# Two more tiles of a feed-forward layer as seven block products, with the work around them moved

## The chip, the cores and the metric

The kernel runs on one core of a Trainium2 chip. The metric is device time in microseconds (us): the median of several executions. One further execution is recorded by the hardware profiler. Its page and its trace are what is read here. The engines are called as in the profile: PE is TensorE (matmuls), PEld its weight loads, DVE is VectorE, ACT is ScalarE, POOL is GpSimd, and SP issues most of the DMAs.

## The reference

One layer of a streaming encoder (model width 1024) is computed for two groups of columns: 1024 positions of a new stream and 32 of a running one. A modulated input goes through one input projection into three kinds of heads, their outputs through an output projection and a layer norm; then comes a gated feed-forward layer of width 2816 and a second layer norm. The change lies in the feed-forward layer:

```python
x = _layer_norm(ALPHA * x + (1 + g1) * mix, ln1_g, ln1_b)
h = x * (1 + sc2) + sh2
y = (jax.nn.silu(h @ w_gate) * (h @ w_up)) @ w_down
x = _layer_norm(ALPHA * x + (1 + g2) * y, ln2_g, ln2_b)
```

`silu(v)` is `v * sigmoid(v)`. All of it is float32.

## The kernel before

**Layout.** Activations lie transposed: 128 partitions by 8 blocks `k` of the model width, with positions along the free axis. The 1056 positions are cut into group 0 (512 columns) and group 1 (544 columns). Every product of a weight `W` and an activation `x` is made of three matmuls on rounded parts, `W_hi x_hi + W_hi x_lo + W_lo x_hi` (function `gemm`, lines L130, L131, L132). Weights are loaded in float32, cast to their high part by ACT (L117) and split off to their low part by DVE (L118).

**The feed-forward stage.** `w_gate` and `w_up` are cut into 22 tiles `j` of 128 output rows (`FF = 22`). The function `up` makes one such tile directly: for each of its two column ranges a gate product and an up product over 8 blocks `k`, then `silu` on ACT and DVE (L1310 to L1315), which leaves the high and low part of the tile's activation. In group 1 the ranges are 0 to 272 and 272 to 544, so a direct tile has 2 matrices x 8 blocks x 3 parts x 2 ranges = 96 matmuls of 272 columns.

The function `sup` makes the same tile from seven block products (a scheme of Strassen's kind for a 2 by 2 block matrix with four `k` blocks each): 7 x 4 x 3 = 84 matmuls. For that it needs sums of weight blocks and sums of activation blocks. The weight sums are formed partly in advance, in DRAM, by `sums()`: SP copies one block (L90, tile name `start_dp`), and a DMA issued by POOL adds another onto it (L1333). The rest of a tile's weight sums are two DVE additions (L1387, L1388), and three casts and splits (L1381, L1382). The activation sums, called the operand `T`, are formed once by `sup_operand`: the feed-forward input was stored to DRAM block by block (`start_dh<-lna_tmp`), and is loaded back in pairs (blocks `k` and `k+4`); for each of four pairs DVE makes four additions of 272 columns (L1356 to L1359) and two splits of 544 (L1362). The seven products are combined by DVE (L1408 to L1422), out of two PSUM tags that alternate.

In group 1, tiles 0, 1 and 2 are direct (`SJ = 3`), 3 to 20 go by block products, and the last one (`TS = 1`) is direct.

**Order of the work.** Group 0 runs the whole feed-forward layer first, then group 1. Tiles are taken in `GROUPS` of 3, 3, 4, 4, 4 and 4; one tile beyond a group is made before the group's `down` product, which adds `w_down` times the tiles' activations into the residual `z` (DVE updates at L1212). So for group 1: tiles 0 to 3, down of tiles 0 to 2, tiles 4 to 6, down of tiles 3 to 5, and so on.

Two pieces of work are tied to the place where group 0 ends and group 1 begins. First, the last `down` of group 0 calls `ln_sum` for each of its outputs: ACT squares `z` (L1073), DVE adds the squares into `qs` (L1074), POOL adds `z` into `zs` (L1083). Two matmuls with a matrix of ones make means of these (`ln_means`, L1095, tile `lnb_t`), from which the second layer norm of group 0 (`ln2`, a generator `norm0`) goes on, step by step, behind tiles from 3 on, as the list `turns` says. Second, `ln1_res(1)` scales and shifts group 1's residual, 16 instructions `tensor_scalar` on POOL (L1268), each 128 by 272; `down` of group 1 adds onto them later.

Each engine runs its own queue in order; waits are semaphores on other engines and DMAs. The order within each queue is made by a scheduler from the program's dependences and from a model of time; `issue_after` adds an order without a wait.

Of the kernel before, what the change touches and what calls it, by code (L numbers as in the profile page):

```python
# [15 lines left out]
P = 128  # L16
D = 1024
KT = 8
# [28 lines left out]
FF = 22  # L47
SJ = 3
TS = 1
# [19 lines left out]
class Kernel:  # L69
    def __init__(self, ctx, tc, d):  # L70
        self.ctx, self.tc, self.nc, self.d = ctx, tc, tc.nc, d
        self.n = 0
        self.phase = "start"

    def pool(self, name, bufs=1, ctx=None, **kw):
# [22 lines left out]
    def tie(self, ins, target, engines):  # L98
        for i in ins:
            if i.engine in engines and "DMA" not in type(i).__name__ and "Dma" not in type(i).__name__:  # L100
                self.tc.add_manual_dep(i, target.ins.name, mybir.DependencyInfo(
                    mybir.DependencyClass.NoSync, mybir.DependencyReason.SCHED_ONLY), reason="order")

    def weights(self, src, nk, ncol, eng=None, pool=None):
# [958 lines left out]
    def ln_sum(self, st, z, m, sl):  # L1063
# [5 lines left out]
        if st["last"] and m != o[7]:  # L1069
            sq = self.t((self.pg, self.pu)[m % 2], [P, 512], F32, self.utag[m % 2])[:, :sl.stop - sl.start]  # L1070
        else:
            sq = self.t(self.p2, [P, 272], F32, "tmp", 4)[:, :sl.stop - sl.start]
        nc.scalar.activation(sq, z[:, m, sl], AF.Square)  # L1073
# [187 lines left out]
    def ln1_res(self, c):  # L1261

        self.phase = f"lna{c}"
        for a, b in MM[c]:
            for k in range(KT):
                zk = self.z[c][:, k, a:b]
# [3 lines left out]
                else:  # L1270
                    self.nc.scalar.activation(zk, zk, AF.Identity, bias=self.colp[:, 56 + k:57 + k],
                                              scale=self.colp[:, 48 + k:49 + k])

    def ln_consts(self):
# [59 lines left out]

    def sup_operand(self, ks):

# [6 lines left out]
        def load(k):  # L1343
            self.phase = "sup"
            x, y = ((self.t(self.px, [P, 544], F32, z, 1) for z in ("c", "uv")) if k % 2 else
                    (f(self.t(self.px, [P, 544], F32R, z, 1)) for z in ("w2h", "w2l")))
# [3 lines left out]

        loaded = {k: load(k) for k in ks[:2]}
        yield
        for k in ks:
# [6 lines left out]
            for z, (h, l) in zip((x, y), self.T):  # L1360
                nc.scalar.copy(h[:, k], z)
                tt(l[:, k], z, f(h[:, k]), ALU.subtract)  # L1362
            if k + 2 in ks:
                loaded[k + 2] = load(k + 2)
            yield
# [219 lines left out]
    def run(self):  # L1585
# [147 lines left out]
        with ExitStack() as s7:  # L1733
            pq = self.pool("pq", ctx=s7)
            for u, h in enumerate(range(PRE, 8)):
                self.fm_unit(w3[1 + h], self.evac_qk(h, True), (1,))
                if u:
                    self.ada((18 + 2 * u, 19 + 2 * u), pq, "late", 6, self.pt, "t")
        self.ln1_res(0)
        s1.close()  # L1740
# [9 lines left out]
        for g, (j0, nj) in enumerate(GROUPS):  # L1750
# [31 lines left out]
            else:  # L1782
                self.down(0, g, act, WIDE)
        st.update(pivot=False, sum=True)
        self.down(0, last, act, MM[0], st)
        self.ln1_res(1)
        self.st0 = st
# [3 lines left out]
        self.px = self.pool("px")  # L1791
        operand = self.sup_operand(range(4))
        next(operand)
# [5 lines left out]
        norm0 = norm0()  # L1799
        turns = [1, 1, 2, 2, 2, 1] * 2  # L1800
        for g, (j0, nj) in enumerate(GROUPS):
            for j in range(j0 + (g > 0), min(j0 + nj + (g < last), FF - TS)):
                if self.nsum <= FF:
                    self.sums()
                if j >= SJ:
                    self.sup(j, act, pa)
                    with tc.issue_after(self.lastact.ins):
                        for _ in range(turns.pop(0) if turns else 0):
                            next(norm0, None)
                    continue  # L1810
                for i, _ in enumerate(self.up(1, j, act, pa, MM[1])):
                    if 0 < 2 * j + i // 2 < 5 and i % 2:
                        with tc.issue_after(self.lastact.ins):
                            next(operand, None)
            if g < last:
# [135 lines left out]
```

## Time and profile before

| | us |
|---|---|
| median of 3 runs | 1334.09 (1333.72 to 1335.16) |
| the profiled execution | 1336.75 |
| its span, first to last instruction | 1334.6 |

The mean granted clock of PE was 0.997. On one core every engine's time line can be read directly: the span, then who is busy, then who waits for whom. Times in the quoted rows count from the span's start. In PE's rows, the end of group 0's last `down` comes at about 946.5 us, tiles 0 to 3 of group 1 follow until about 993, and the `down` of tiles 0 to 2 after them.

### The profile page before, as it was taken

The page shows a single profiled execution, that of the slowest core. Times are in us where ns is not written, and L with a number is a line of the kernel's source. Part 1 is how long each engine was busy: PE and PEld are TensorE (multiplying, and loading weights), DVE is VectorE, ACT ScalarE, POOL GpSimd, SP SyncE. Part 2 cuts the span into 40 slices and gives each one's busy share as a digit, 9 for nine tenths or more (in the row PEclk, how much of TensorE's full clock was granted, in tenths as well). Part 3 has the DMA queues.
Part 4 walks back from the last instruction along what each step waited for, and adds up shares of the span by engine and source line. Part 5 has one row for each costly group of instructions (what it writes and reads, how often), then busy time and mean ns, then how long its engine had stood idle before and what let it go on. Part 6 is the DMA issues. An engine that isn't in the chain of part 4 may idle for free.

```text
span 1334.6 us, 24982 instructions
## 1 busy us (share of the span) xinstructions
PE 1319.4 (99%) x9424; PEld 1196.9 (90%) x9424; DVE 989.6 (74%) x2106; ACT 647.2 (48%) x1284; POOL 183.7 (14%) x221
## 2 busy tenths in 40 slices
PE   9999999999999999999999999999999999999996
PEld 6798888978999888888887888999999999999996
DVE  4636666667778677777777676778998997978677
ACT  3424456443537645455354454436754463635344
POOL 0101100011305000000000001134600000000423
PEclk9999999999999999999999999999999999999998
DMA  9775555533748655354343334663786866644311
GB/s 362 276 257 167 182 180 180 152 130 111 222 169 258 186 136 147 112 163 115 111 139 108 102 104 129 202 146 113 207 219 161 233 177 188 177 139 136 102 49 67
DMA packets 118135, 217.43 MB, mean 163 GB/s; under 512 B 18340, under 2 KB 62496, under 8 KB 118016
## 3 DMA queue, kind: packets, MB, share of 16 engines
q1 hardware_dynamic: 111200, 204.37, 48.9%
q0 software_dynamic: 5616, 10.86, 4.9%
q8 instruction: 74, 1.21, 0.4%
q10 hardware_dynamic: 1200, 0.62, 0.2%
q14 instruction: 45, 0.37, 0.1%
HBM read 184.95 MB, written 50.77 MB: 177 GB/s over the span
## 4 chain that ended last, share of the span: by engine, by line
PE 90%; DMA 4%; DVE 3%; ACT 1%; issue 1%; SPq 0%; DVEq 0%; ACTq 0%
PE up_g L132 6%; PE up_g L130 6%; PE up_g L131 6%; PE dn_g L132 4%; PE dn_g L130 4%; PE dn_g L131 4%; PE tm_g L404 3%; PE tm_g L406 3%; PE tm_g L405 3%; PE sup_u L132 3%; PE sup_u L131 3%; PE sup_u L130 3%; PE wo_g L132 2%; PE wo_g L130 2%; PE fox_t L938 2%; PE wo_g L131 2%
## 5 line engine op out<-in xcount | busy, mean ns | idle before, releaser
L131 PE MATMUL up_g<-ada_al,up_whi 128*128 128x512 f32 (+1 forms) x384 | 140.4, 366 | 0.0
L132 PE MATMUL up_g<-ada_ah,up_wlo 128*128 128x512 f32 (+1 forms) x384 | 140.2, 365 | 0.0
L130 PE MATMUL up_g<-ada_ah,up_whi 128*128 128x512 f32 (+1 forms) x384 | 140.0, 365 | 0.0
L1381 ACT CAST sup_whi<-sup_raw 128x1024 fp32r<-128x1024 f32 x54 | 56.5, 1050 | 99.0 <-PE dn_u L131 39.9
L117 ACT CAST up_whi<-up_raw 128x1024 fp32r<-128x1024 f32 x50 | 52.5, 1050 | 68.1 <-PE dn_g L131 35.8
L130 PEld LDWEIGHTS up_g<-ada_ah,up_whi 128*128 128x128 f32 x384 | 72.4, 188 | 11.5 <-issue 0.4
L131 PEld LDWEIGHTS up_g<-ada_al,up_whi 128*128 128x128 f32 x384 | 72.4, 188 | 11.1
L1382 DVE TENSOR_TENSOR sup_wlo<-sup_raw,sup_whi 128x1024 fp32r<-128x1024 f32 x54 | 69.1, 1279 | 17.6 <-ACT sup_whi L1381 17.6
L132 PEld LDWEIGHTS up_g<-ada_ah,up_wlo 128*128 128x128 f32 x384 | 72.5, 189 | 10.7
L1212 DVE SCALAR_TENSOR_TENSOR wo_z<-dn_g,start_mod,wo_z 128x512 f32<-128x512 f32 (+4 forms) x120 | 60.2, 521 | 22.7 <-PE dn_g L132 22.3
L911 ACT ACTIVATE fox_p<-fox_s,fox_fmx 128x384 f32<-128x384 f32 (+2 forms) x96 | 55.1, 578 | 44.8 <-DVE fox_fmx L909 25.2
L130 PE MATMUL dn_g<-up_acth,dn_whi 128*128 128x512 f32 (+2 forms) x200 | 73.7, 369 | 1.5 <-DVE wo_z L1212 1.5
L132 PE MATMUL dn_g<-up_acth,dn_wlo 128*128 128x512 f32 (+2 forms) x200 | 73.6, 368 | 0.0
L131 PE MATMUL dn_g<-up_actl,dn_whi 128*128 128x512 f32 (+2 forms) x200 | 73.4, 368 | 0.0
L118 DVE TENSOR_TENSOR up_wlo<-up_raw,up_whi 128x1024 fp32r<-128x1024 f32 x50 | 65.1, 1302 | 8.9 <-ACT up_whi L117 7.9
L906 DVE TENSOR_REDUCE fox_fmx<-fox_s 128x1 f32<-128x384 f32 (+2 forms) x96 | 53.1, 554 | 22.3 <-PE fox_s L903 21.0
L117 ACT CAST dn_whi<-dn_raw 128x1024 fp32r<-128x1024 f32 (+1 forms) x44 | 42.7, 971 | 49.8 <-PE up_g L131 33.6
L943 ACT CAST fox_pth<-fox_t 128x512 fp32r<-128x512 f32 (+1 forms) x80 | 41.5, 542 | 42.9 <-PE fox_t L938 42.0
L118 DVE TENSOR_TENSOR dn_wlo<-dn_raw,dn_whi 128x1024 fp32r<-128x1024 f32 (+1 forms) x44 | 49.5, 1125 | 9.8 <-ACT dn_whi L117 9.7
L944 DVE TENSOR_TENSOR fox_ptl<-fox_t,fox_pth 128x512 fp32r<-128x512 f32 (+1 forms) x80 | 49.8, 632 | 6.9 <-ACT fox_pth L943 6.5
L1333 POOL DMA_DIRECT2D start_dp<-w_gu x19 | 19.8, 1042 | 222.8 <-DMA start_dp<-w_gu 222.8
L404 PE MATMUL tm_g<-tm_whi,start_ah 128*128 128x264 f32 (+2 forms) x160 | 49.8, 312 | 0.0
(695 smaller groups left out, 4677.9 us busy)
## 6 DMA issues: line engine op xcount, KB each, us to landing
up_raw<-w_gu SPq DMA_DIRECT2D x50, 512.0 KB
ada_late<-w_ada SPq DMA_DIRECT2D x28, 512.0 KB
dn_raw<-w_dn SPq DMA_DIRECT2D x28, 512.0 KB
sup_raw<-w_gu SPq DMA_DIRECT2D x20, 512.0 KB
start_dp<-w_gu SPq DMA_DIRECT2D x19, 512.0 KB
start_dp<-w_gu POOLq DMA_DIRECT2D x19, 512.0 KB, 8.8
wo_raw<-w_o SPq DMA_DIRECT2D x18, 512.0 KB
sup_raw<-start_dp SPq DMA_DIRECT2D x18, 512.0 KB
```

The costliest lines, as they stand in the source:

```text
L117: nc.scalar.copy(hi[:, :w], raw[:, :w])
L118: (eng or nc.vector).tensor_tensor(lo[:, :w], raw[:, :w], f(hi[:, :w]), ALU.subtract)
L130: nc.tensor.matmul(ps, hi, xh(k), start=start and k == 0, stop=False)
L131: nc.tensor.matmul(ps, hi, xl(k), start=False, stop=False)
L132: self.lastmm = nc.tensor.matmul(ps, lo, xh(k), start=False, stop=stop and k == n - 1)
L404: nc.tensor.matmul(ps[:, :ncol], xh, hi, start=k == 0, stop=False)
L906: nc.vector.tensor_reduce(mxs[:, x:x + 1], s[:, :w], AX.X, ALU.max, negate=True)
L911: nc.scalar.activation(pr[:, lo:hi], banks[x][:, :hi - lo], AF.Exp, bias=mxs[:, 0:1], accum_out=sums[:, x:x + 1])
L944: nc.vector.tensor_tensor(pl[:, :e], ps[:, :e], f(ph[:, :e]), ALU.subtract)
L1212: self.lastz = self.nc.vector.scalar_tensor_tensor(z[:, m, x:y], ps[:, x - a:y - a], g[i], z[:, m, x:y], ALU.mult, ALU.add)
L1381: nc.scalar.copy(h, x)
L1382: tt(l, x, f(h), ALU.subtract)
```

## The change

Tiles 1 and 2 of group 1 go by `sup` (`SJ = 1`). The operand `T` is then wanted behind tile 0, so all eight of its loads are issued at once, two of them into buffers of tile activations, and it is formed within tile 0. The sums of group 0 (`ln_sum`) no longer stand in its last `down`: a generator `sum0` emits them behind tiles 4 to 7, four outputs each (`SUMS`), and the norm's steps follow from tile 6 on (`TURNS`). Group 1's residual instructions are emitted behind tiles 0, 1 and 2 (`RES`: 6, 5, 5). A new function `behind` gives every POOL instruction of these two pieces a real wait on `lastT`, the last DVE instruction of the operand. One more `sums()` stands ahead of group 0's last `down`.

```diff
-SJ = 3
+SJ = 1
+SUMS = (0, 0, 0, 4, 4, 4, 4)
+TURNS = (0, 0, 0, 0, 0, 2, 2, 2, 2, 2, 2, 2, 2, 2)
+RES = (6, 5, 5)
...
+    def behind(self, first):
+
+        for i in self.nc.cur_bb.bb.instructions[first:]:
+            if i.engine == mybir.EngineType.Pool:
+                self.tc.add_manual_dep(i, self.lastT.ins.name, mybir.DependencyInfo(
+                    mybir.DependencyClass.Sync, mybir.DependencyReason.DATA), reason="behind")
...
-            sq = self.t(self.p2, [P, 272], F32, "tmp", 4)[:, :sl.stop - sl.start]
+            pool, w, tag, n = (self.px, 256, "sq", 1) if st is self.st0 else (self.p2, 272, "tmp", 4)
+            sq = self.t(pool, [P, w], F32, tag, n)[:, :sl.stop - sl.start]
...
-        for a, b in MM[c]:
-            for k in range(KT):
+        for k in range(KT):
+            for a, b in MM[c]:
+                self.phase = f"lna{c}"
...
+                yield
...
-            x, y = ((self.t(self.px, [P, 544], F32, z, 1) for z in ("c", "uv")) if k % 2 else
+            x, y = ((self.t(self.px, [P, 544], F32, z, 1) for z in ("c", "uv")) if k == 1 else
+                    (f(self.t(pool, [P, 544], F32R, z, 5)) for z in ("acth", "actl")) if k else
...
-        loaded = {k: load(k) for k in ks[:2]}
+        loaded = {k: load(k) for k in ks}
...
-                tt(l[:, k], z, f(h[:, k]), ALU.subtract)
-            if k + 2 in ks:
-                loaded[k + 2] = load(k + 2)
+                self.lastT = tt(l[:, k], z, f(h[:, k]), ALU.subtract)
...
-        st.update(pivot=False, sum=True)
+        st.update(pivot=False)
+        self.sums()
         self.down(0, last, act, MM[0], st)
-        self.ln1_res(1)
...
-        turns = [1, 1, 2, 2, 2, 1] * 2
+        def sum0():
+            for a, b in MM[0]:
+                for m in range(KT):
+                    self.phase = "dn0"
+                    first = len(nc.cur_bb.bb.instructions)
+                    self.ln_sum(self.st0, self.z[0], m, slice(a, b))
+                    self.behind(first)
+                    yield
+
+        def res():
+            for _ in self.ln1_res(1):
+                self.behind(len(nc.cur_bb.bb.instructions) - 1)
+                yield
...
                     self.sup(j, act, pa)
+                    for _ in range(RES[j] if j < len(RES) else 0):
+                        next(res, None)
                     with tc.issue_after(self.lastact.ins):
+                        for _ in range(sums.pop(0) if sums else 0):
+                            next(sum0, None)
                         for _ in range(turns.pop(0) if turns else 0):
                             next(norm0, None)
                     continue
                 for i, _ in enumerate(self.up(1, j, act, pa, MM[1])):
-                    if 0 < 2 * j + i // 2 < 5 and i % 2:
-                        with tc.issue_after(self.lastact.ins):
-                            next(operand, None)
+                    next(operand, None)
+                if j == 0:
+                    for _ in operand:
+                        pass
+                    for _ in range(RES[0]):
+                        next(res, None)
```

Lines move by 4 to 14 in the changed file: `gemm` is L141 to L143, the residual L1280, the additions into `zs` L1095, the means L1107, the accumulations L1346, the operand's splits L1376.

How the queues move is read from their order. On PE before, where tile 3 ends (`sup_u`) and the `down` of group 1's tiles 0 to 2 begins (`dn_g`), both means of group 0 (`lnb_t`) stand between the two:

```order
L130 MATMUL sup_u_11760<-lna_ah_11196,sup_w2h_11663 128x272
L131 MATMUL sup_u_11760<-lna_al_11197,sup_w2h_11663 128x272
L132 MATMUL sup_u_11760<-lna_ah_11196,sup_w2l_11664 128x272
L1095 MATMUL lnb_t_11777<-up_zs_9536,start_onesm_136 128x256
L1095 MATMUL lnb_t_11779<-up_qs_9537,start_onesm_136 128x256
L130 MATMUL dn_g_11796<-up_acth_11208,dn_whi_11792 128x272
L131 MATMUL dn_g_11796<-up_actl_11209,dn_whi_11792 128x272
L132 MATMUL dn_g_11796<-up_acth_11208,dn_wlo_11793 128x272
```

On PE of the change, at the same place (`dn_u`, `dn_g` are the first two of the down product's accumulators; the six rows of each have the activations of tile 0, `up_act`, and tile 1, `sup_act`):

```order
L143 MATMUL sup_u_11720<-dn_ah_11126,sup_w2l_11624 128x272
L141 MATMUL dn_u_11766<-up_acth_11146,dn_whi_11739 128x272
L142 MATMUL dn_u_11766<-up_actl_11147,dn_whi_11739 128x272
L143 MATMUL dn_u_11766<-up_acth_11146,dn_wlo_11740 128x272
...
L141 MATMUL dn_g_11743<-sup_acth_11315,dn_whi_11739 128x272
L142 MATMUL dn_g_11743<-sup_actl_11316,dn_whi_11739 128x272
L143 MATMUL dn_g_11743<-sup_acth_11315,dn_wlo_11740 128x272
L1107 MATMUL lnb_t_12401<-up_zs_9538,start_onesm_138 128x256
L141 MATMUL dn_g_11754<-up_acth_11146,dn_whi_11739 128x272
```

The mean of `zs` for the first column range now stands behind the first twelve matmuls of the `down` product and ahead of all the others; the mean of `qs` is no longer beside it (it comes in the next `down`).

On POOL before, from the output projection's sums (`wo_zs`) on, residuals (`wo_z` with `start_colp`) and additions into `up_zs` take turns:

```order
L1083 TENSOR_TENSOR wo_zs_9892<-wo_zs_9892,wo_z_1851_9895 128x272 x10
L1233 TENSOR_TENSOR wo_z_1851_9895<-wo_z_1851_9895,wo_qs_9893 128x272 x2
L1268 TENSOR_SCALAR wo_z_1851_9895<-wo_z_1851_9895,start_colp_107 128x272 x8
L1083 TENSOR_TENSOR up_zs_9536<-wo_z_836_4579 128x256
L1233 TENSOR_TENSOR wo_z_1851_9895<-wo_z_1851_9895,wo_qs_9893 128x272 x2
L1083 TENSOR_TENSOR up_zs_9536<-up_zs_9536,wo_z_836_4579 128x256
L1268 TENSOR_SCALAR wo_z_1851_9895<-wo_z_1851_9895,start_colp_107 128x272
```

On POOL of the change, from the same place to the next accumulation after it:

```order
L1095 TENSOR_TENSOR wo_zs_9894<-wo_zs_9894,wo_z_1853_9897 128x272 x6
L1245 TENSOR_TENSOR wo_z_1853_9897<-wo_z_1853_9897,wo_qs_9895 128x272 x2
L1346 DMA start_dp_17_73<-w_gu 256x1x512
L1245 TENSOR_TENSOR wo_z_1853_9897<-wo_z_1853_9897,wo_qs_9895 128x272 x2
L1346 DMA start_dp_16_72<-w_gu 256x1x512
L1346 DMA start_dp_19_75<-w_gu 256x1x512
L1280 TENSOR_SCALAR wo_z_1853_9897<-wo_z_1853_9897,start_colp_109 128x272 x16
L1095 TENSOR_TENSOR up_zs_9538<-wo_z_838_4581 128x256 x2
L1095 TENSOR_TENSOR up_zs_9538<-up_zs_9538,wo_z_838_4581 128x256 x12
L1346 DMA start_dp_20_76<-w_gu 256x1x512
```

All 16 residuals now stand behind three accumulations and ahead of all 14 additions; the first residual waits for `lastT` on DVE, so all that stands behind it does too.

On DVE of the change, `lastT` is the last split into `dn_al`; ahead of it come the split of tile 2's first weights (`sup_wlo`), behind it tile 2's first weight sum and the combination of tile 1 (`sup_uv`):

```order
L1394 TENSOR_TENSOR sup_wlo_11467<-sup_raw_11460,sup_whi_11466 128x1024
L1420 TENSOR_TENSOR sup_sil_11342<-sup_g_11359,sup_tmp_11341 128x272
L1376 TENSOR_TENSOR dn_al_11127<-sup_acth_11140,dn_ah_11126 128x544
L1376 TENSOR_TENSOR dn_al_11127<-sup_actl_11137,dn_ah_11126 128x544
L1326 TENSOR_TENSOR up_sil_11218<-up_u_11267,up_sil_11218 128x272
L1376 TENSOR_TENSOR dn_al_11127<-sup_actl_11141,dn_ah_11126 128x544
L1399 TENSOR_TENSOR sup_raw_11460<-sup_raw_11460,sup_raw_11461 128x512
L1328 TENSOR_TENSOR up_actl_11147<-up_sil_11218,up_acth_11146 128x272
L1421 TENSOR_TENSOR sup_uv_11343<-sup_tmp_11341,sup_u_11373 128x272
```

The whole operand is thus complete while the last range of tile 0 is still being evacuated (`up_u`, `up_actl`); before, its last split came beside the evacuation of tile 2.

More of the change, by code (lines that the diff above doesn't have):

```diff
@@ L73, in __init__ @@
         self.phase = "start"
+        self.st0 = None
     def pool(self, name, bufs=1, ctx=None, **kw):
@@ L1261, in ln1_res @@
     def ln1_res(self, c):
-        self.phase = f"lna{c}"
-        for a, b in MM[c]:
-            for k in range(KT):
+        for k in range(KT):
+            for a, b in MM[c]:
+                self.phase = f"lna{c}"
                 zk = self.z[c][:, k, a:b]
@@ L1333, in sums, with sup_operand @@
             self.nc.gpsimd.dma_start(self.dp[i - 1], blocks(i - 1)[:, 0:4:3], accum_op=ALU.add)
-    def sup_operand(self, ks):
+    def sup_operand(self, ks, pool):
         nc = self.nc
@@ L1738, in run @@
                     self.ada((18 + 2 * u, 19 + 2 * u), pq, "late", 6, self.pt, "t")
-        self.ln1_res(0)
+        for _ in self.ln1_res(0):
+            pass
         s1.close()
@@ L1791, in run @@
         self.px = self.pool("px")
-        operand = self.sup_operand(range(4))
+        operand = self.sup_operand(range(4), pa)
         next(operand)
@@ L1799, in run @@
         norm0 = norm0()
-        turns = [1, 1, 2, 2, 2, 1] * 2
+        def sum0():
[10 more added lines that the diff above has]
+                yield
+        sum0, res = sum0(), res()
+        sums = list(SUMS)
+        turns = list(TURNS)
         for g, (j0, nj) in enumerate(GROUPS):
@@ L1811, in run @@
                 for i, _ in enumerate(self.up(1, j, act, pa, MM[1])):
-                    if 0 < 2 * j + i // 2 < 5 and i % 2:
-                        with tc.issue_after(self.lastact.ins):
-                            next(operand, None)
+                    next(operand, None)
+                if j == 0:
+                    for _ in operand:
+                        pass
+                    for _ in range(RES[0]):
+                        next(res, None)
             if g < last:
```

## The prediction

> **What bounds the kernel now.** I read the page first: its head, the busy line, and the chain that ended last.
>
> ```profile
> span 1334.6 us, 24982 instructions
> ...
> PE 1319.4 (99%) x9424; PEld 1196.9 (90%) x9424; DVE 989.6 (74%) x2106; ACT 647.2 (48%) x1284; POOL 183.7 (14%) x221
> ...
> PE 90%; DMA 4%; DVE 3%; ACT 1%; issue 1%; SPq 0%; DVEq 0%; ACTq 0%
> ```
>
> TensorE is busy for 1319.4 of 1334.6 us and holds 90% of the chain: time is won only by issuing fewer matmuls, and any wait put into PE's stream counts in full. The view of PE's waits says where it waited between 900 and 1060 us, the stretch in which the change lies:
>
> ```profile
> PE dn_g L130 <- DVE wo_z L1212: 1.5, 1, 1.5
> ```
>
> One wait of 1.5 us. How much room the other engines have there is read from the windows (columns: PE, PEld, DVE, ACT, POOL busy, granted clock, DMA share, GB/s):
>
> ```profile
> 940.00:950.00 10.00, 10.00 (x86) 10.00 (x85) 10.00 (x20) 7.45 (x18) 10.00 (x11) 1.00 0.80 257
> 950.00:960.00 10.00, 10.00 (x82) 10.00 (x81) 9.12 (x14) 5.57 (x16) 7.49 (x10) 1.00 0.88 218
> ...
> 980.00:990.00 10.00, 10.00 (x82) 10.00 (x81) 9.96 (x20) 7.30 (x14) 1.04 (x1) 1.00 0.78 206
> 990.00:1000.00 10.00, 10.00 (x79) 9.90 (x78) 8.57 (x18) 5.23 (x9) 1.03 (x1) 1.00 1.04 258
> ...
> 1020.00:1060.00 40.00, 40.00 (x322) 40.00 (x321) 37.02 (x70) 21.58 (x33) 3.09 (x3) 1.00 0.68 193
> ...
> 1100.00:1200.00 100.00, 100.00 (x801) 100.00 (x800) 82.84 (x153) 44.30 (x63) 5.16 (x5) 1.00 0.60 170
> ```
>
> PE is full, but VectorE is nearly full too (10.00, 9.12, 9.96 of 10), and GpSimd is full in 940 to 950 and almost idle from 960 on. So DVE has no slack where the change adds work to it, and POOL's work of 940 to 957 is what is moved.
>
> **The change part by part.**
>
> *24 matmuls fewer.* A direct tile is 96 matmuls of 272 columns, a block-product tile 84. Two tiles give 24. The last window row has 801 matmuls in 100.00 us, 0.125 us each: **−3.0 us**, 0.22% of the span. PE's rows in the order agree (8392 before, 8368 now).
>
> *DVE in tiles 0 to 3.* The DVE timeline gives every duration as start to next start, back to back and with POOL idle:
>
> ```profile
> 983.94 1.22 DVE L1382 TENSOR_TENSOR sup_wlo<-sup_raw,sup_whi 128x1024 fp32r<-128x1024 f32 x1
> 985.07 0.43 DVE L1359 TENSOR_TENSOR sup_uv<-sup_c,sup_uv 128x272 f32<-128x272 f32 x1
> 985.42 0.69 DVE L1382 TENSOR_TENSOR sup_w2l<-sup_w,sup_w2h 128x512 fp32r<-128x512 f32 x1
> 986.03 0.72 DVE L1362 TENSOR_TENSOR lna_al<-sup_c,lna_ah 128x544 fp32r<-128x544 f32 x1
> 986.66 0.44 DVE L1312 TENSOR_TENSOR up_sil<-up_g,up_sil 128x272 f32<-128x272 f32 x1
> 987.01 0.96 DVE L118 TENSOR_TENSOR dn_wlo<-dn_raw,dn_whi 128x768 fp32r<-128x768 f32 x1
> 987.88 0.73 DVE L1362 TENSOR_TENSOR lna_al<-sup_uv,lna_ah 128x544 fp32r<-128x544 f32 x1
> ```
>
> That is 1.13 us for 1024 columns, 0.61 for 512, 0.87 for 768, 0.63 for 544, 0.35 for 272. In the changed order DVE has, between the last update of group 0's down product and the operand's last instruction (the one that GpSimd is now tied to), 3 of 1024, 2 of 512, 8 of 544 and 25 of 272 columns: 3.4 + 1.2 + 5.0 + 8.8 = 18.4 us. The update cannot come before PE's last matmul of that product at about 946.5; with half a us behind it, DVE could be through at 947.0 + 18.4 = 965.4 if nothing were late. The operand's blocks go through DRAM, and the chain of waits has both halves of that trip:
>
> ```profile
> 944.54 5.62 DMA start_dh<-lna_tmp
> 950.59 3.17 DMA start_dh<-lna_tmp
> ...
> 988.00 15.00 DMA sup_raw<-w_gu
> ```
>
> Store and load took 5.62 + 3.17 = 8.8 us where DMA was 80% busy. The last block is now wanted about 4 us after its store, so DVE can stand up to some 5 us; SP's order now has none of the block sums' copies among the operand's transfers, where two stood before, so I take half, 2.5: operand complete at **968**, between 965.4 and 970.
>
> From there to the last instruction of tile 3's evacuation but one, DVE has 5 of 1024, 7 of 512, 4 of 768, 10 of 544 and 15 of 272 columns: 5.7 + 4.3 + 3.5 + 6.3 + 5.3 = 25.1 us, to 993. PE alone needs 96 + 3 × 84 = 348 matmuls, 43.5 us from 946.5, to 990.0. DVE is 3 us later; the accumulators that the down product begins with are freed one by one, so not all of it reaches PE: **+1.5 us**, between 0 and 4.
>
> *The wait that is added.* PE's order now has the mean of group 0's sums (L1107, `lnb_t<-up_zs`) twelve matmuls into the down product of group 1, and behind it all the rest of that product. It needs 13 of GpSimd's 14 additions. These stand in POOL's queue behind the 16 residual instructions, and those behind the operand's last one on DVE; before, all were done by 957.4, 35 us ahead of PE. Their durations:
>
> ```profile
> 900.72 0.77 POOL L1083 TENSOR_TENSOR wo_zs<-wo_zs,wo_z 128x272 f32<-128x272 f32 x1 [2.37 <-DVE wo_z L1212]
> ...
> 913.17 9.14 POOL L1268 TENSOR_SCALAR wo_z<-wo_z,start_colp 128x272 f32<-128x272 f32 x8 [1.41 <-ACT lna_tmp L1236]
> ...
> 936.57 0.57 POOL L1268 TENSOR_SCALAR wo_z<-wo_z,start_colp 128x272 f32<-128x272 f32 x1 [0.43 <-ACT lna_tmp L1236]
> ...
> 956.22 1.14 POOL L1083 TENSOR_TENSOR up_zs<-up_zs,wo_z 128x256 f32<-128x256 f32 x1
> ...
> 975.48 1.06 POOL L1333 DMA_DIRECT2D start_dp<-w_gu  x1 [14.57 <-DMA start_dp<-w_gu]
> ```
>
> ```profile
> L1268 POOL TENSOR_SCALAR wo_z<-wo_z,start_colp 128x272 f32<-128x272 f32 x16 | 18.5, 1161 | 1.8 <-ACT lna_tmp L1236 1.8
> L1083 POOL TENSOR_TENSOR up_zs<-up_zs,wo_z 128x256 f32<-128x256 f32 x12 | 12.9, 1085 | 0.8 <-DVE wo_z L1212 0.8
> ```
>
> A residual took 0.57 us alone and 1.14 (9.14 / 8) in a row beside a full DVE; an addition 0.77 and 1.085. From 968 DVE is full again, so I take the contended rows: 968 + 16 × 1.14 + 13 × 1.085 = 968 + 18.2 + 14.1 = **1000.3**. PE gets there at 946.5 + 43.5 + 1.5 + 12 × 0.125 = **993.0**. **PE waits 7.3 us**. With the uncontended rows POOL is done at 968 + 9.1 + 10.0 = 987.1 and PE waits for nothing; that is the lower end, and the nearest rows, under the same load, are the contended ones. One more instruction of POOL's stands ahead: the accumulation of block sums 8, whose copy SP issues behind tile 3's weights; row 975.48 shows such a wait. If it came last, the start would be up to 972 instead of 968 and the wait 11 us.
>
> *The clock.* What an idle PE costs beyond the gap, only the end of the run shows:
>
> ```profile
> 0.00:4.00 4.00, 2.82 (x13) 2.82 (x14) 2.46 (x17) 1.50 (x2) 1.89 (x12) 1.00 0.43 94
> ...
> 1320.00:1325.00 5.00, 4.01 (x23) 2.91 (x21) 3.17 (x9) 2.33 (x7) 2.86 (x4) 1.00 0.08 28
> 1325.00:1330.00 5.00, 0.00 (x0) 0.00 (x0) 4.66 (x13) 3.01 (x7) 2.84 (x5) 0.72 0.17 56
> ```
>
> PE's last matmul ends near 1324.0, and the granted clock of the next 5 us is 0.72: it fell to one half at about 1327.2, 3.2 us after. A wait of 7.3 us reaches that point. If full speed came back only after as long, 3.2 us of matmuls at half speed would cost 1.6 us. The first row, where PE starts at 1.00, says nothing; the resumption is shown nowhere. I take 0, the row of a starting PE being the nearest, and keep 1.6 for the range. The Trainium skill, "TensorE: Matmul & The Clock Gate", part 1, has a rule for it: after an idle window of about 3.4 us PE runs at half speed, until it has been busy for about as long. That would be 1.7 us lost and my sum 1340.1 (an estimate from that page). The trace agrees on the fall (3.2 us); on the return no row bears, and the first row speaks against a cold start.
>
> *The gap that goes.* The 1.5 us wait of PE at 1004.3 hangs on a load that took 15.00 us (row 988.00 above), issued into a DMA share of 1.04. With PE held up before it, that load has several us more, and DVE's z updates behind it too: **−1.5 us**, at worst 0.
>
> *The rest.*
>
> ```profile
> 954.29 4.03 DVE L1074 TENSOR_TENSOR up_qs<-up_qs,dn_tmp 128x256 f32<-128x256 f32 x3 [0.88 <-ACT dn_tmp L1073]
> ```
>
> These are three of the 14 additions of squares; they leave this place (where one of them stood still beside GpSimd's additions) and come at tiles 4 to 7, where DVE has 37.02 of 40 us; the norm's steps that stood there move on into a stretch with 82.84 of 100, under full cover of PE: 0, at worst +2 if DVE runs out (its one buffer for squares ties ACT and DVE in turn). Block sums 7 are now formed before the output projection's last weights, their copy ahead of two weight loads on SP: 0, at worst +1.
>
> Sum: −3.0 + 1.5 + 7.3 − 1.5 = **+4.3 us**. The profiled execution took 1336.75 us (span 1334.6 and 2.15 around it), 2.66 above the median of 1334.09; it becomes 1341.05. From the median: **1338.4 us**, slower by 0.3%.
>
> **The rivals.**
>
> *GpSimd is in time.* The additions and residuals run near their rows alone (0.57, 0.77), PE meets finished sums. For it: the residual at 936.57 did take only 0.57. Against: eight in a row took 1.14 each. It decides at a mean of 25 us / 29 = 0.86 us per instruction. Then −3.0 + 1.5 − 1.5 = −3.0: **1331.1**, 1329.6 if DVE delays nothing. This is the other side, faster.
>
> *GpSimd is in time at DVE's cost.* These two rows are 1024-column splits beside GpSimd additions:
>
> ```profile
> 946.29 1.67 DVE L118 TENSOR_TENSOR up_wlo<-up_raw,up_whi 128x1024 fp32r<-128x1024 f32 x1
> ...
> 950.42 1.76 DVE L118 TENSOR_TENSOR up_wlo<-up_raw,up_whi 128x1024 fp32r<-128x1024 f32 x1
> ```
>
> They take 0.45 to 0.54 us longer than 1.22. Thirteen additions at 0.46 are 6 us on an engine that is already behind; with half of it on PE, −3.0 + 1.5 + 3.0 − 1.5 = 0: **1334.1**.
>
> *Each loses to the other.* If every GpSimd instruction sat out a whole DVE one (25.1 us / 41 = 0.61), residuals would cost 1.18 and additions 1.38; with the late start of 972 that ends at 972 + 18.9 + 17.9 = 1008.8, a wait of 15.8 less the 1.6 that I would then also charge the clock for: −3.0 + 1.5 + 15.8 + 1.6 − 1.5 = +14.4; without the late start +10.4: **1344.5**. The Trainium skill, "SBUF — State Buffer", section "Who interferes with whom", says this: a DVE instruction with two SBUF inputs and a GpSimd instruction that reads SBUF exclude each other for a whole instruction. The residual rows agree (1.14 beside splits of 1.13); the addition rows (1.085) fall short of it.
>
> That the matmuls do not go is no rival: the order has 24 rows fewer.
>
> **How the numbers follow.** Forecast (a wait of 4 to 11 us) 0.38; GpSimd in time 0.35; in time at DVE's cost 0.15; each loses 0.12. What a measurement of this kernel can tell from no change is about 0.2%, 2.7 us: faster is below 1331.4, slower above 1336.8. Faster: 0.30 of the second case. Same: its other 0.05, 0.12 of the third, 0.03 of the forecast's small waits, 0.20. Slower: 0.35 of the forecast, 0.03 of the third, 0.12 of the last, 0.50. Cases of both signs hold most of the chance: the forecast's own range is 1335.1 to 1343.7, from a wait of 4 us to one of 11 with the clock's 1.6 on top. The range is 1329.6, GpSimd in time with DVE's whole cover, to 1344.5.
>
> **What would show it.** In the changed profile: PE waits for L1107's input from POOL around 993 for about 7 us (right), or its list of waits has no POOL entry (second case), or DVE entries instead (third). The 16 residuals begin near 968 and last 18 us. The wait at 1004.3 is gone. The granted clock in the 5 us behind the wait is below 1.00, or not. I am wrong if the operand is complete well before 965, or if residuals take under 0.8 us each.

## The result, and the profile after

| | before | changed |
|---|---|---|
| median, us | 1334.12 (1333.72 to 1335.57, 6 runs) | 1349.07 (6 runs); 1349.03 for the five of them at 1347.34 to 1349.15 |
| ratio | | 1.0105, 95% interval 1.0094 to 1.0116 |

The change makes the kernel about 14 us slower: the sign that was forecast, at three times the size, and outside the range. The sixth execution took 2613 us with its matmuls at half rate from end to end; it is left out of the ratio, as is one of 4927 us of an experiment, of which there is no trace, and since it was the recorded one, the profile read here is of a second series of the same kernel (`e1_again`: median 1347.56 us; the recorded execution 1347.15, span 1345.2). In the changed kernel's numbering L1095 is the addition L1083 of before, L1280 the residual L1268, L1376 the operand's split L1362, L1394 the weight split L1382, L1346 the accumulating DMA L1333.

The head and the busy line of its page:

```profile
span 1345.2 us, 24941 instructions
...
PE 1320.4 (98%) x9400; PEld 1197.3 (89%) x9400; DVE 992.6 (74%) x2120; ACT 651.6 (48%) x1282; POOL 188.8 (14%) x223
...
PE 91%; DMA 3%; POOL 2%; DVE 2%; issue 1%; ACT 1%; SPq 0%; DVEq 0%; ACTq 0%; POOLq 0%
```

PE runs 24 matmuls fewer, and yet is busy a microsecond longer: a first sign that some of them ran slowly. POOL, which had no share in the chain that ended last, now holds 2% of it. The view of PE's waits, the rows of the stretch from 849 us on (us in total, times, longest):

```profile
PE lnb_t L1107 <- POOL up_zs L1095: 8.7, 1, 8.7
...
PE sup_u L142 <- DVE dn_al L1376: 1.1, 1, 1.1
PE sup_g L143 <- DVE sup_wlo L1394: 0.8, 1, 0.8
...
PE wo_g L142 <- DVE up_al L1165: 0.5, 1, 0.5
```

The first is the wait that the prediction added, 8.7 us for 7.3. The next two are PE waiting in tile 1 for DVE, once for a split of the operand (`dn_al`) and once for a weight split (`sup_wlo`) that stands among the operand's instructions; the prediction did not have them. The windows of the same execution (PE, PEld, DVE, ACT, POOL busy, granted clock, DMA share, GB/s) give what each is worth:

```profile
940.00:950.00 10.00, 10.00 (x86) 10.00 (x85) 7.53 (x16) 6.28 (x16) 0.00 (x0) 1.00 0.66 210
950.00:960.00 10.00, 10.00 (x82) 10.00 (x81) 7.20 (x17) 4.58 (x8) 0.77 (x1) 1.00 0.88 259
960.00:970.00 10.00, 8.02 (x48) 7.40 (x48) 10.00 (x20) 6.57 (x13) 0.28 (x1) 0.83 0.81 201
970.00:980.00 10.00, 10.00 (x82) 10.00 (x82) 9.60 (x16) 6.03 (x9) 9.01 (x8) 1.00 0.58 101
980.00:990.00 10.00, 10.00 (x82) 10.00 (x82) 10.00 (x15) 6.68 (x10) 10.00 (x8) 1.00 0.53 154
990.00:1000.00 10.00, 5.91 (x48) 5.70 (x46) 9.93 (x14) 4.80 (x7) 10.00 (x11) 0.96 0.97 313
1000.00:1010.00 10.00, 5.38 (x24) 5.20 (x25) 1.08 (x3) 0.00 (x0) 8.32 (x11) 0.53 0.57 133
```

A full window holds 82 matmuls, 0.122 us each. Two places fall short: 960 to 970, where 34 are missing (4.1 us), and 990 to 1010. DVE is idle for 2.5 and 2.8 us in the first two windows, then full; POOL has nothing but one DMA to issue (at 959) until 971, and is then full without a break until 1008. The tie to the operand has moved all its work to there, and its time line shows it:

```profile
971.00 1.04 POOL L1346 DMA_DIRECT2D start_dp<-w_gu  x1 [10.71 <-DMA start_dp<-w_gu]
971.60 20.63 POOL L1280 TENSOR_SCALAR wo_z<-wo_z,start_colp 128x272 f32<-128x272 f32 x16
992.20 2.72 POOL L1095 TENSOR_TENSOR up_zs<-wo_z 128x256 f32<-128x256 f32 x2
994.89 10.36 POOL L1095 TENSOR_TENSOR up_zs<-up_zs,wo_z 128x256 f32<-128x256 f32 x12
```

16 residuals took 1.29 us each, and 13 additions some 12.3 us behind them. The 12.3 are of two kinds: the first eight, beside a busy DVE, took 1.12 us from start to start, those behind 1001, where DVE had run out of work, 0.68. PE stops at 995.9 and goes on at 1004.6, when the thirteenth is through.

### The profile page after: what moved, and what is told of

It is laid out like the page before. It is cut to its first block, busy times and chain, and to the rows that moved or that the text cites. A ratio compares the mean times of both kernels' runs of the same rounds, so it can differ in the third digit from the quotient of the medians.

```text
span 2611.1 us, 24941 instructions
## 1 busy us (share of the span) xinstructions
PE 2595.5 (99%) x9400; PEld 2179.1 (83%) x9400; DVE 1015.7 (39%) x2120; ACT 662.6 (25%) x1282; POOL 166.9 (6%) x223
## 4 chain that ended last, share of the span: by engine, by line
PE 99%; issue 0%; DVE 0%; ACT 0%; DVEq 0%; ACTq 0%
PE up_g L143 6%; PE up_g L142 6%; PE up_g L141 6%; PE dn_g L143 5%; PE dn_g L141 5%; PE dn_g L142 4%; PE tm_g L415 4%; PE tm_g L416 3%; PE tm_g L417 3%; PE sup_u L142 3%; PE sup_u L143 3%; PE sup_u L141 3%; PE fox_t L949 3%; PE wo_g L141 2%; PE wo_g L142 2%; PE wo_g L143 2%
## 5 line engine op out<-in xcount | busy, mean ns | idle before, releaser
L142 PE MATMUL up_g<-ada_al,up_whi 128*128 128x512 f32 (+1 forms) x384 | 235.1, 612 | 0.0
L141 PE MATMUL up_g<-ada_ah,up_whi 128*128 128x512 f32 (+1 forms) x384 | 233.9, 609 | 0.0
L143 PE MATMUL up_g<-ada_ah,up_wlo 128*128 128x512 f32 (+1 forms) x384 | 233.9, 609 | 0.0
L142 PEld LDWEIGHTS up_g<-ada_al,up_whi 128*128 128x128 f32 x384 | 121.2, 316 | 42.8 <-issue 39.3
L141 PEld LDWEIGHTS up_g<-ada_ah,up_whi 128*128 128x128 f32 x384 | 119.2, 310 | 41.9 <-issue 37.6
L143 PEld LDWEIGHTS up_g<-ada_ah,up_wlo 128*128 128x128 f32 x384 | 120.6, 314 | 39.1 <-issue 34.8
L141 PE MATMUL dn_g<-up_acth,dn_whi 128*128 128x512 f32 (+2 forms) x184 | 117.5, 640 | 0.0
L143 PE MATMUL dn_g<-up_acth,dn_wlo 128*128 128x512 f32 (+2 forms) x184 | 116.2, 632 | 0.0
L949 PE MATMUL fox_t<-start_ident,fox_p 128*128 128x128 f32 x288 | 87.4, 439 | 0.0
L417 PE MATMUL tm_g<-tm_whi,start_al 128*128 128x264 f32 (+2 forms) x160 | 80.1, 501 | 0.0
L416 PE MATMUL tm_g<-tm_wlo,start_h1h 128*128 128x264 f32 (+2 forms) x160 | 79.8, 499 | 0.0
L1394 DVE TENSOR_TENSOR sup_wlo<-sup_raw,sup_whi 128x1024 fp32r<-128x1024 f32 x60 | 74.7, 1247 | 13.1 <-ACT sup_whi L1393 12.6
L416 PE MATMUL tm_g<-tm_wlo,start_ah 128*128 128x264 f32 (+2 forms) x160 | 79.5, 497 | 0.0
L415 PE MATMUL tm_g<-tm_whi,start_h1h 128*128 128x264 f32 (+2 forms) x160 | 79.2, 495 | 0.0
L417 PE MATMUL tm_g<-tm_whi,start_h1l 128*128 128x264 f32 (+2 forms) x160 | 79.1, 495 | 0.0
```

Of the source, the lines that this page charges most:

```text
L141: nc.tensor.matmul(ps, hi, xh(k), start=start and k == 0, stop=False)
L142: nc.tensor.matmul(ps, hi, xl(k), start=False, stop=False)
L143: self.lastmm = nc.tensor.matmul(ps, lo, xh(k), start=False, stop=stop and k == n - 1)
L415: nc.tensor.matmul(ps[:, :ncol], xh, hi, start=k == 0, stop=False)
L416: nc.tensor.matmul(ps[:, :ncol], xh, lo, start=False, stop=False)
L417: self.lastmm = nc.tensor.matmul(ps[:, :ncol], xl, hi, start=False, stop=k == 7)
```

## The experiments

Two theories stood first. One: the time goes into the late sums on POOL, and PE standing for them. The other: it goes into the two tiles themselves (an operand and weight sums that DVE cannot deliver in time), and the POOL wait only hides that. The expectations name a third, a single wait of PE of over 8 us near 965 for the operand on its way back from DRAM; the rows above (1.1 and 0.8 us) rule it out in that form. The short diffs are against the changed kernel unless another is named.

**The changed kernel again, and the kernel before again.** Each was profiled a second time, so that a single execution does not carry the comparison.

> The changed kernel itself, for a profile of an ordinary execution. All theories expect about 1348 us (+14 on before). Theory 1 (the forecast's step, mis-sized): PE has one wait at the mean of group 0's sums (L1107) for POOL's additions, near 993 us, of 12 to 15 us, and the granted clock falls behind it. Theory 2 (VectorE cannot feed tiles 1 to 3): several waits of PE on DVE or ACT between 950 and 1000 us, 12 to 15 us together, none on POOL over 3 us. Theory 3 (the operand comes back from DRAM late): one wait of PE near 965 us on the operand's casts or splits (L1375, L1376), over 8 us.

> The kernel before, once more with a profile. Its first profiled execution was 2.66 us above its median and had a wait of 1.5 us of PE at 1004 us, for which the prediction counted 1.5 us won. If that wait is part of the kernel, it is here again, and the span is near 1334.6. If it belonged to that one execution, the span is near 1332.0 (median less 2.15) and PE waits nowhere between 900 and 1060 us; then the 1.5 us were never there to win.

Measured: 1347.56 us (1347.15 to 1347.97), ratio 1.0098, interval 1.0078 to 1.0119; and 1334.36 us with a span of 1332.3. The list of PE's waits of the kernel before, from its top:

```profile
PE start_o L294 <- DVE start_onesm L161: 1.2, 1, 1.2
PE ada_t L202 <- DMA start_araw<-w_ada: 0.8, 2, 0.6
PE ada_t L211 <- ACT ada_adas L206: 0.6, 1, 0.6
PE fox_o L946 <- DVE fox_ptl L944: 0.5, 1, 0.5
```

All of these belong to earlier stages. The 1.5 us wait at 1004.3, which the prediction struck off as a gain, is not in this execution: it belongs to the one that was recorded first, and the median, from which the forecast was counted, need not hold it. Three of its windows:

```profile
960.00:970.00 10.00, 10.00 (x82) 10.00 (x82) 9.31 (x21) 7.41 (x15) 0.00 (x0) 1.00 0.86 190
...
990.00:1000.00 10.00, 10.00 (x79) 9.89 (x79) 8.23 (x17) 4.89 (x10) 1.79 (x2) 1.00 0.97 293
1000.00:1010.00 10.00, 10.00 (x82) 10.00 (x82) 9.54 (x23) 3.87 (x5) 0.27 (x1) 1.00 0.93 233
```

Against these, the changed kernel has 34 matmuls fewer in the first and 31 + 58 = 89 fewer in the other two: 4.1 and 10.9 us.

**The sums untied.** One line out of `sum0`; the residuals stay tied behind the operand.

```diff
                     self.ln_sum(self.st0, self.z[0], m, slice(a, b))
-                    self.behind(first)
                     yield
```

> The additions of group 0's sums are no longer held behind the operand's last instruction (the residual still is); on POOL all 14 now stand ahead of the residuals, and the first mean stands in the middle of tile 1 on PE. Theory 1: the wait goes, 1330 to 1336 us. Theory 2: DVE is as late as before and has POOL's additions beside the operand as well: 1346 to 1350. Theory 3: 1346 to 1350.

Measured: 1336.54 us, ratio 1.0016 (1.0006 to 1.0026), span 1333.3. POOL's time line, from the group of additions on:

```profile
946.73 5.37 POOL L1095 TENSOR_TENSOR up_zs<-up_zs,wo_z 128x256 f32<-128x256 f32 x5 [0.84 <-DVE wo_z L1224]
960.42 1.05 POOL L1346 DMA_DIRECT2D start_dp<-w_gu  x1 [8.32 <-DMA start_dp<-w_gu]
971.15 1.04 POOL L1346 DMA_DIRECT2D start_dp<-w_gu  x1 [9.69 <-DMA start_dp<-w_gu]
971.96 21.83 POOL L1280 TENSOR_SCALAR wo_z<-wo_z,start_colp 128x272 f32<-128x272 f32 x16
```

The additions are done at 952.1, and the first mean, which now stands in the middle of tile 1 on PE, runs at 964.3 without waiting for them; the residuals start as late as ever (971.96) and last even longer, and nobody minds. Its windows at the two places:

```profile
960.00:970.00 10.00, 8.07 (x57) 7.04 (x56) 10.00 (x20) 6.98 (x13) 1.05 (x1) 1.00 0.84 210
...
990.00:1000.00 10.00, 10.00 (x82) 10.00 (x81) 9.12 (x18) 5.97 (x8) 5.83 (x6) 1.00 0.98 305
1000.00:1010.00 10.00, 10.00 (x82) 10.00 (x81) 9.48 (x22) 2.65 (x3) 0.66 (x1) 1.00 0.80 202
```

The second place is whole again, so the tie of 14 additions is worth 10.9 us there. The first has 57 matmuls for 48: 9 x 0.122 = 1.1 us more. Together 12.0 us, and the spans differ by 11.9. The first theory holds for the bulk. What is left beside before (2.1 us, while the matmuls saved are worth 2.9) belongs to the second: the operand's wait, here 25 matmuls or 3.1 us, and one more place, below.

**The mean later, the sums as late.** The two matmuls that want the sums are put behind the whole down product on PE.

```diff
+        if c == 0:
+            self.tie(nc.cur_bb.bb.instructions[start:], self.dnmm, (mybir.EngineType.PE,))
```

> The changed kernel with one more order on PE: group 0's means stand behind the first down product of group 1 (384 matmuls, some 48 us, later than in the change). Nothing else is moved. Theory 1: PE no longer meets unfinished sums, 1330 to 1336 us. Theory 2 and theory 3: the waits stand elsewhere, 1345 to 1349 us.

Measured: 1338.8 us, ratio 1.0044 (1.0024 to 1.0065), above the 1330 to 1336 that were expected; seven of ten executions lie between 1336.2 and 1339.9 and three between 1345 and 1347. PE waits for POOL nowhere now, though POOL's additions run to 1006.9, later than in the changed kernel. So in most executions late sums cost some 2 us more than the untied ones; the rest of the 10.9 comes from a consumer of theirs that stands ahead of a long product in PE's queue. Why three executions still took 1345 is not shown: the recorded one was of the shorter kind.

**The residuals untied, the sums still tied.** The `behind` in `res` is taken out.

> The mirror of the untied sums: the 16 residuals are free of the operand and stand ahead of it on POOL, the 14 additions still wait for it. The first mean comes 72 matmuls earlier on PE than in the change, about 986 us. If the wait is the sum of start, residuals and additions on POOL (971 + 20.6 + 12.3 = 1004 in the change), the additions now end near 971 + 13 x 1.0 = 984 and PE waits for nothing or up to 2 us: 1336 to 1339 us. If the additions' own tie to the operand were enough for the loss, it stays over 1343.

Measured: 1338.87 us, ratio 1.0041 (1.0023 to 1.0059): six executions at 1336.9 to 1339.0 and three at 1345.6 to 1349.2. Here the recorded one was a long one. PE's longest wait, and then the time lines of DVE and of POOL around it:

```profile
PE sup_u L141 <- ACT sup_whi L1393: 7.3, 1, 7.3
```

```profile
975.31 9.59 DVE L1400 TENSOR_TENSOR sup_raw<-sup_raw 128x512 f32<-128x512 f32 x1
```

```profile
974.29 1.91 POOL L1095 TENSOR_TENSOR up_zs<-wo_z 128x256 f32<-128x256 f32 x2
976.07 8.27 POOL L1095 TENSOR_TENSOR up_zs<-up_zs,wo_z 128x256 f32<-128x256 f32 x12
```

PE does not wait for POOL, the sums being done at 984.3. It waits for a cast on ACT, which waits for one DVE addition of 512 columns, which took 9.59 us where the same instruction took 0.68 in the changed kernel. It ended when POOL's twelve additions ended. So the 14 additions in a run stop PE either way: behind the residuals by coming late, ahead of them by shutting out a DVE instruction in this execution. Two more of the nine have times like it, but no profile.

**The moves alone.** Block products from tile 3 on as before (`SJ = 3`), with the moved sums, turns and operand; ten of the 16 residual instructions are left out, since they were emitted behind block-product tiles 1 and 2.

> SJ = 3 again: tiles 1 and 2 of group 1 direct, with all moves of the change kept (late sums and norm, residual spread and tied, operand within tile 0). The means then stand behind tile 6 on PE, far behind POOL's additions. Theory 1: no wait, 1333 to 1336 us, as before. Theory 2: DVE has its slack of direct tiles back, 1333 to 1336. Theory 3: the operand is wanted only at tile 3, 1333 to 1336. If it is over 1340, the moves themselves cost the time, and none of the three theories holds as put.

Measured: 1336.08 us, ratio 1.0014 (1.0004 to 1.0023). PE has no wait for POOL: the sums and means come behind tiles 6 to 9 here, the first mean at 1082.6, and POOL's additions were done at 996.6. The moves gain nothing by themselves; the recorded execution is eight matmuls short between 950 and 960 us, about 1 us.

**One tile instead of two.** Two kernels with `SJ = 2`: the changed one with its sums untied (all of the operand's steps still in tile 0), and the kernel before.

> Tile 1 direct again (SJ = 2), so 12 matmuls fewer than before and not 24, and the sums untied as in the run before; the residual stays tied and is complete. The operand is wanted 12 us later. Theory A (with SJ = 1 what is left of the loss is PE's wait for the operand near 962 us and the half clock behind it, 3.5 to 4.2 us): those go, and 1.5 us are won on the kernel before, 1332 to 1334 us. Theory B (the moved sums and norm cost 1.5 to 2 us later on, wherever the operand stands): 1334.5 to 1336.5.

> The kernel before with SJ = 2 and the operand formed within tiles 0 and 1; sums, norm and residual where they were before. Theory A: the operand shares DVE with the sums beside tile 0 and comes late to tile 2, some us of waits: 1333 to 1337. Theory B: no sums moved, 12 matmuls fewer: 1332 to 1333.

Measured: 1337.55 (ratio 1.0018, 1.0008 to 1.0027) and 1337.12 (1.0017, 1.0008 to 1.0026). With 12 matmuls fewer, no late sums and a tile's length more time for the operand, both are still 2 to 3 us slower than before; the first is above both of its expectations, the second just above the upper end of its own. In these two kernels there is a price on the one tile, and much of it stands in the tiles that have to form the operand: the first is 33 matmuls short between 950 and 970 (4.0 us; PE waits 2.2 us for DVE there, granted clock 0.93 and 0.89), the second 15 between 970 and 990 (1.8 us). The windows 849 to 860, in the output projection, 85 us ahead of any changed tile, show one part of it; first the changed kernel, then the kernel before, then the moves alone, then the kernel before with `SJ = 2`:

```profile
849.00:860.00 11.00, 10.42 (x80) 9.90 (x79) 8.62 (x17) 6.77 (x15) 0.00 (x0) 1.00 0.65 196
```

```profile
849.00:860.00 11.00, 11.00 (x88) 10.87 (x86) 8.66 (x18) 6.84 (x14) 0.00 (x0) 1.00 0.63 184
```

```profile
849.00:860.00 11.00, 11.00 (x89) 10.92 (x88) 8.52 (x18) 6.86 (x14) 0.00 (x0) 1.00 0.59 174
```

```profile
849.00:860.00 11.00, 10.09 (x79) 9.64 (x78) 8.74 (x20) 7.43 (x16) 0.00 (x0) 1.00 0.58 161
```

Every kernel so far with a block product ahead of tile 3 has 77 to 80 matmuls there, those with `SJ = 3` 88 or 89: 8 to 10 matmuls, about 1 us. On SP's queue the changed kernel has a row that before has not:

```profile
830.59 0.43 SPq L90 DMA_DIRECT2D sup_w<-w_gu  x1
831.06 0.63 SPq L94 DMA_DIRECT2D start_dp<-w_gu  x1
835.81 0.33 SPq L90 DMA_DIRECT2D wo_raw<-w_o  x1
```

This is a copy for a block sum: it follows the third load of the first block-product tile, which the scheduler has hoisted to 830.6, and goes ahead of loads that the output projection wants.

**Without the early copy.** The copies follow a tile's second load instead of its third. Three kernels: the one with the sums untied; `SJ = 2` with the sums untied and the operand's steps spread over tiles 0 and 1; and the kernel before with `SJ = 2`.

```diff
+        first = self.lastload
         self.load(raw[2], self.d["w_gu"][j][:, 1536:])
+        self.lastload = first
```

> The kernel with the group-0 sums untied from the operand (1336.54 us), and one more edit: SyncE's copies for the block sums follow the second load of a block-product tile instead of its third, so none of them is issued among the output projection's loads at 831 us. Theory A: that early copy (0.63 us of SP's queue and its bytes ahead of w_o and dmix loads) is what makes the output projection 1.2 us longer in every kernel with a block-product tile before tile 3: 1335.3, and 88 matmuls again between 849 and 860 us, where there were 80. Rival B: the longer stage comes from another part of the new order of loads; 1336.5, and 80 matmuls.

> Block products from tile 2 on (one tile more than before the change, one less than after it), the operand's four steps spread over tiles 0 and 1 as before the change, sums untied, residuals still tied behind the operand, no early copy. Theory A (the 1.2 us of the output projection is the early copy; the 2.2 us that PE waited in tile 0 in the run with all steps there came from their crowding): 1337.55 - 1.2 - 2.0 = 1334.3, the same as before; if the matmuls saved by one tile (1.5 us) come through in full, 1333.3. Rival B (the gain of a tile is taken by other waits whatever is spread): 1336.5 or more.

> The kernel before with block products from tile 2 on (1337.12 us), and without the early copy for the block sums. Theory A: 1337.12 - 1.2 = 1335.9. Rival B: 1337.1.

Measured: 1339.72 (ratio 1.0042, 1.0028 to 1.0056), 1334.65 (1.0004, 0.9995 to 1.0013) and 1336.89 (1.0023, 1.0013 to 1.0033). The window 849 to 860 of the first:

```profile
849.00:860.00 11.00, 11.00 (x90) 10.96 (x88) 8.38 (x17) 6.86 (x14) 0.00 (x0) 1.00 0.56 155
```

The output projection is whole again, 90 matmuls (90 and 87 in the other two): the early copy was the cause there. And yet the first kernel is 3 us slower for it, and the third only 0.2 us faster where 1.2 were expected (it is now 35 matmuls short between 970 and 990, for 15 with the copy): two misses. For the first, the view of DVE's waits shows where the time goes:

```profile
DVE sup_uv L1370 <- DMA sup_uv<-start_dh: 4.2, 1, 4.2
DVE sup_w2l L1370 <- DMA sup_w2l<-start_dh: 3.0, 1, 3.0
```

The copies now fall at 926 and 946 us, among the stores and loads of the operand; DVE stands 7.2 us for the operand's loads, against 1.6 in the kernel with the sums untied, and PE waits 5.7 us in tile 1, with the granted clock at 0.82 and 0.84: from 960 to 980 it is 78 matmuls short, where the kernel with the sums untied is 28 short. That the copies lengthen these round trips is read from their place in the queue; no run shows it alone. For this kernel, the 1 us in the output projection was the cheaper place. The second kernel comes out even with before, near its expectation of 1334.3: with the operand spread over two tiles, no matmul is missing for it between 950 and 980. It still has a wait, here PE's row and the DVE row ahead of it:

```profile
PE dn_u L141 <- DVE wo_z L1224: 1.5, 1, 1.5
```

```profile
936.07 3.66 DVE L1245 TENSOR_TENSOR wo_z<-wo_z,wo_qs 128x272 f32<-128x272 f32 x1
```

Its neighbours of the same form took 0.43 us. POOL ran four `TENSOR_TENSOR` back to back from 936.05 to 939.4 (two into `wo_z`, two of the sums), over most of these 3.66 us: the same sight as the 9.59 us above, on a smaller scale. None of the kernels beats the kernel before.

## Why the prediction was wrong

**Which steps failed.** The wait for POOL, the largest term, came as it was put. The operand's term failed: the lateness was charged 1.5 us at the end of tile 3, and PE stood for it inside tile 1, for 4.1. The clock's term failed: it was put at nothing, on a row that was misread, and is 2.2 us behind the wait. The gap counted as a gain was not there to win, and the copy put at nothing cost 1.0.

**The matmuls that go: right.** 24 fewer, 2.9 us at this execution's 0.122.

**The wait that is added: the mechanism right, three sizes off.** Operand, then 16 residuals, then 13 additions, then PE: all as put. The forecast was 968 + 18.2 + 14.1 = 1000.3; it became 971.6 + 20.6 + 12.3 = 1004.6. Residuals beside a full DVE took 1.29 us, more than the 1.14 of the contended row; additions 0.95 on the mean, less than 1.085, because DVE ran out of work behind 1001 (1.12 before that, 0.68 after). That the two errors nearly cancel is luck. POOL was 4.3 us later than forecast, PE 2.9 (995.9 for 993.0): so 8.7 instead of 7.3. The two rivals in which GpSimd is in time fell: it would have taken 0.86 us per instruction, and 33.0 / 29 = 1.14 were measured. The rival in which each loses fell too: its wait was 11.8 us or more.

**The operand: wrong in its place and its size.** The prediction let DVE be 3 us late at the end of tile 3 and charged 1.5. In fact PE waited inside tile 1, where the first block products read the operand's parts one by one; that reader was not priced at all. The view of DVE's waits in the changed kernel:

```profile
DVE sup_w2l L1370 <- DMA sup_w2l<-start_dh: 2.8, 1, 2.8
DVE sup_uv L1370 <- DMA sup_uv<-start_dh: 2.4, 1, 2.4
```

The prediction saw this trip through DRAM, allowed "up to some 5 us" for it and took half. DVE stood 5.2, the upper end. The last block that it stood for was there at 955.2, and 16.1 us of its work lay between that and the operand's end at 971.4. With the sums untied DVE stood only 1.6, being busy until then, but that block was there at 955.7, with the residuals untied at 957.6, without the early copy at 963.2, and each time the operand ended some 16 us later: it is this block's return from DRAM that sets it. PE's first block products lost 34 matmuls by it, 4.1 us instead of 1.5. Of these, the run with the sums untied shows 3.1 without any fall of the clock.

**The clock: taken as 0, it is 2.2 us behind the wait and some 1.1 more at the operand.** Fine windows of the changed kernel (PE busy, count, granted clock among the columns):

```profile
998.00:999.00 1.00, 0.00 (x0) 0.00 (x0) 0.97 (x2) 0.94 (x2) 1.00 (x2) 1.00 0.95 348
999.00:1000.00 1.00, 0.00 (x0) 0.00 (x0) 1.00 (x2) 0.00 (x0) 1.00 (x3) 0.57 0.98 399
...
1005.00:1009.00 4.00, 4.00 (x17) 3.82 (x17) 0.00 (x0) 0.00 (x0) 3.32 (x4) 0.50 0.53 53
1009.00:1010.00 1.00, 1.00 (x9) 1.00 (x8) 0.14 (x1) 0.00 (x0) 0.00 (x0) 0.81 1.11 199
```

PE's last matmul ended at 995.9, the clock fell to one half 3.2 us later, as at the end of the run before, and it came back only at about 1009.4, 4.8 us after PE went on: 17 matmuls in 4 us instead of 33. With 89 missing matmuls (10.9 us) and 8.7 of standing, 2.2 us are the clock's (the 1.1 at the operand are within its 4.1). The choice of 0 leaned on the first 4 us of the run, whose granted clock reads 1.00. The matmuls of that row say otherwise. These are the same instruction at the start of the kernel before and a few us later:

```profile
1.18 4.64 PE L294 MATMUL start_o<-start_onesm 128*128 128x128 f32 x20 [1.18 <-DVE start_onesm L161]
...
8.54 2.62 PE L294 MATMUL start_o<-start_onesm 128*128 128x128 f32 x22
```

20 took 4.64 us, then 22 took 2.62: PE started at about half rate, which the column does not show. Read so, the row is one of a PE that comes from standing, and 4.64 less 20 times 0.119 would have charged 2.3 us. The Trainium skill, "TensorE: Matmul & The Clock Gate", part 1, says that the gate needs a busy window of some 3.4 us, counted by a free-running clock, before it opens; the 4.8 us here agree with it, the rest of a window and then a whole one. The prediction named this rule, priced it at 1.7 and set it aside, which the measurement does not bear out.

**The gap that goes: −1.5 forecast, 0 found.** One recorded wait of one execution was booked as the kernel's.

**The rest: the early copy, taken as 0 and at worst 1, is 1.0.** Eight matmuls in the window 849 to 860.

The sum by measured terms: −2.9 + 4.1 + 8.7 + 2.2 + 0 + 1.0 = +13.1 us; the spans of the two profiled executions differ by 12.9. (The first series' median lies 1.9 us above the recorded execution; no profile shows that rest.) Beside the forecast's +4.3, the error is 2.6 for the operand, 2.2 for the clock, 1.5 for the gap, 1.4 for the wait and 1.0 for the copy: five small terms, all to one side. The range failed because its upper end charged the wait's worst case and 1.6 for the clock and left the others at their middle: with the prediction's own worst cases for the operand (2.5 more), the gap (1.5) and the rest (3) the forecast's 1343.7 would have been 1350.7. The one case that came near, +14.4, was worked out and left outside the range, and its wait of 15.8 us is not what happened.

What stays open is why the changed kernel's clock fell in tile 1 in the recorded execution and not in that of the untied sums, with the same waits there (PE busy 8.02 and 8.07), and what makes the two kernels above fall into one of two times.

## What to carry to other kernels

A tie that holds back one engine's work is priced by who reads that work, and where that reader stands in its own queue: 14 additions cost 10.9 us because one small matmul wanted them ahead of a long product, and some 2 where nothing waited for them. Ask, too, where the first reader of late work stands: the operand was late for tile 1, not for tile 3. Price an idle gap of a matmul engine with its clock, and take the clock from the matmuls' own times; strike a wait off as a gain only when a second execution shows it too. When several terms each have a small worst case on the same side, the range must add them up.

## What the runs showed of the hardware

A two-input DVE instruction can be held for a whole run of GpSimd instructions, not for one: one of 0.68 us took 9.59 beside the last 13 of 14 additions on POOL, one of 0.43 took 3.66 beside four of POOL's instructions. In the changed kernel DVE instructions beside the same additions were only slowed (1.14 us for 0.68, 1.18 and 1.24 for 0.72). Two kernels here took times of two values, some 8 to 10 us apart; one recorded long execution shows the hold, and that it makes the others long is argued, not shown. The Trainium skill, "SBUF — State Buffer", section "Who interferes with whom", says that the two contend for a shared read interface under an exclusive lock; the runs agree that they contend, and these two records look as if the one that loses can lose many times in a row.

In the changed kernel the same addition on POOL took 1.12 us beside a busy DVE and 0.68 once DVE had nothing to do; a residual took 1.29 in a row beside a nearly full DVE, and 0.57 alone in the kernel before: the price of a GpSimd instruction is a matter of what DVE does beside it.
